# A delta-rule scan's triangular inverse cut into two pipeline stages, in 64-column form, and weight tiles' low parts kept in memory

## The chip, the cores and the metric

One NeuronCore of a Trainium2 chip. The metric is device time of one execution in microseconds; lower is better. A core has TensorE (matmuls; weight loads are listed apart), VectorE, ScalarE, GpSimd, and SyncE, which here only issues DMAs. Each takes its instructions in an order fixed when the program is built.

## The reference

One step of a two-layer hybrid decoder, for a prompt of 1024 tokens and for 8 samples of 8 tokens, width 1024. Layer 0 mixes with a convolution module, layer 1 with RWKV-7 time mixing; behind each mixer come attention over 256 memory tokens and a squared-ReLU MLP. The change touches layer 1's mixer:

```python
r = xr @ w_r; k = xk @ w_k; v = xv @ w_v        # x*: six mixes of a token and the token before it
decay, a, g = ...                                # each by a low-rank pair of products
def step(s, inp):                                # per head, s is 64 x 64; 16 heads
    rt, wt, kt, vt, at, bt = inp
    sa = einsum('bhvk,bhk->bhv', s, at)
    s = s * wt[:, :, None, :] + sa[..., None] * bt[:, :, None, :] + vt[..., None] * kt[:, :, None, :]
    return s, einsum('bhvk,bhk->bhv', s, rt)
```

## The kernel before, in words

**Two streams.** The tokens are cut into part 0 (512 prompt tokens) and part 1 (512 prompt tokens and the 64 of the samples). Stream A takes part 0 and stream B part 1 through the layers, each by a Python generator. `pace` advances whichever has the smaller clock; a generator yields an estimated cost, and the scan's bare yields count 1.344 (A) or 1.248 (B). This gives the written order, which is the priority by which the scheduler that builds the program places instructions; the scan's rank 1000 places further ahead (`SCAN_AHEAD`). A's scan must end before B's begins. Beside A's scan B does the end of its first MLP and its projections; beside B's scan A does its part of layer 1 up to the second MLP.

**Weights.** `Stream.load` brings a 128 x 1024 tile into one of four shared raw buffers (L110) and splits it: ScalarE's rounded copy is the high part (L95), VectorE's difference the low part (L96). A product takes three matmuls, high by high, high by low and low by high (L126 to L128). Each stream has a ring of two such tiles, `wt`; the next is loaded when one is taken. Both streams load and split the 24 tiles of w_r, w_k and w_v in `projections`.

**The scan.** It works on chunks of 64 tokens, eight for part 0, and the samples as one more and eight for part 1. `prep` loads a chunk (`ld`, one buffer, L1128), forms decayed keys and queries on VectorE, ScalarE and GpSimd (L1141 to L1178), multiplies them in four passes (L1199) whose results are copied out as `at`, `Aak` and `Aq` (L1202 to L1204), and then makes UV, BK, AV and `bon` (L1210 to L1233). `invert` inverts the unit-triangular 64 x 64 matrix `at` of each of 16 heads: `dg` (L1246, L1248) holds its diagonal 32 x 32 blocks, VectorE inverts the blocks of 16 (L1251 to L1288, giving `td`), and the blocks of 32 and 64 are joined by matmuls of 32 x 32 (L1302 to L1327); the result goes into a 128 x 128 block-diagonal `tt` for each pair of heads (L1329, L1333). `step` takes the state S (L1355), solves with `tt` (L1366) and updates S (L1373 to L1379); `finish` normalises and stores.

`run` works in stages. In each, `together` takes turns, a yield each, between `rest` (step and finish) of one chunk, `inverse` of the next and `prep` of the one behind it. All banks of PSUM that `prep`, `inverse` and the solution use are of one tag, `pp`, with two buffers (`bank("iv")` is one of them too).

Of the kernel before, what the change touches and what calls it, by code (L numbers as in the profile page):

```python
# [17 lines left out]
P = 128  # L18
D = 1024
NC8 = D // P  # L20
# [42 lines left out]
class Stream:  # L63


    def __init__(self, tc, nc, name, side, raw, width):
        self.tc, self.nc, self.name, self.side, self.raw, self.width = tc, nc, name, side, raw, width
        self.turn = self.loads = self.every = 0

# [28 lines left out]
    def load(self, src, cols=1024, rows=P, lo=None, slot=None):  # L98

        if slot is None:  # L100
            slot = self.ring[self.turn % len(self.ring)]
            self.turn += 1
# [9 lines left out]
        wt = pool.tile([P, 2, 1024], F32R, tag=tag, name="wt", bufs=n)  # L112
        self.loads += 1
        if self.every and self.loads % self.every == 0:
            lo = self.nc.gpsimd
        self.split(wt[:rows, 0, :cols], wt[:rows, 1, :cols], raw[:rows, :cols], lo)
        return wt
# [38 lines left out]
def body(tc, nc, es, a, o):  # L156
# [28 lines left out]
    scr = [[dram.tile([P, 6, n], F32, name=f"scr{i}_{m}") for m in range(NC8)] for i, (_, n, _) in enumerate(PARTS)]  # L185
    yg = [dram.tile([P, NC8, n], F32, name=f"yg{i}") for i, (_, n, _) in enumerate(PARTS)]
# [525 lines left out]
    def projections(s, ctx, part, h):  # L712
# [30 lines left out]
        weights = s.weights([(a["rw_w"][i, m], 1024, P) for i in range(3) for m in range(NC8)])  # L743
# [128 lines left out]
        yield from project(2, None, hidden(4, "a", [AF.Copy]), lora("gh", 5))  # L872
        yield from lora("a", 4)
# [193 lines left out]
BUF = dict(w=5, bon=2, at=2, ar=2, Aq=2, UV=2, AV=2, BK=2, pcs=3)  # L1067


def scan(tc, nc, a, o, s, ph, kept, env):  # L1070
# [25 lines left out]
    tts = [filled([P, 8, 128], f"tt{i}", 0.0) for i in range(2)]  # L1096
# [3 lines left out]
    dg = filled([P, 16, 32], "dgz", 0.0)  # L1100
# [29 lines left out]
    def prep(chunk):  # L1130
# [63 lines left out]
        for q in range(2):  # L1194
# [6 lines left out]
            for (h, hs), pa in zip(heads, pas):  # L1201
                nc.scalar.copy(at[hs, cs], pa[:64, :, :64])  # L1202
                nc.vector.tensor_tensor(Aak[64:, cs, h], pa[64:, :, :64], ms[64:], MUL)
                nc.vector.tensor_tensor(Aq[:, cs, h], pa[:, :, 64:], mi, MUL)  # L1204
                yield
# [28 lines left out]
        return dict(chunk=chunk, ar=ar, at=at, Aq=Aq, UV=UV, AV=AV, BK=BK, bon=bon, pcs=pcs)  # L1234
# [7 lines left out]
    def invert(at, tt, deep):  # L1242

        nc.scalar.copy(dg[:, :8], at[:, :, :32])  # L1246
# [42 lines left out]
        td = td[:, :8]  # L1289
# [4 lines left out]
        if deep:  # L1294
# [24 lines left out]
            X = new([P, 256], "W16").rearrange("p (i t) -> p i t", i=8)  # L1319
# [8 lines left out]
        for s in quads:  # L1328
            nc.scalar.copy(tt[s, :, s], td[s])  # L1329
        for h in range(2):  # L1330
            s, s1 = quads[2 * h], quads[2 * h + 1]
            if deep:
                nc.scalar.copy(tt[s, :, s1], pw[s])  # L1333
            else:
                nc.gpsimd.memset(tt[s, :, s1], 0.0)

    def solve(w, pz, cs, n):
# [5 lines left out]
        for g, c in enumerate(range(8)[cs]):  # L1343
            nc.tensor.matmul(pz[:, g, 64:128], lhsT=w["tt"][:, c], rhs=Z[:, g], start=True, stop=True)
# [4 lines left out]
    def step(w, py, S):  # L1349
# [15 lines left out]
        for i in range(8):  # L1365
            nc.tensor.matmul(pu[:, i], lhsT=w["tt"][:, i], rhs=Z[:, i], start=True, stop=True)  # L1366
# [77 lines left out]
    def inverse(n, w):  # L1444
        w["tt"] = tts[n % 2]
        yield from invert(w["at"], w["tt"], w["chunk"] is not None)
        yield
# [38 lines left out]
    def run(chunks):  # L1486
# [4 lines left out]
        if chunks[0] is None:  # L1491
            load_con("rst_s", "rst")
            w = yield from prep(None)
            load_con("rst_p", "rst")
            ready = yield from together(inverse(0, w), prep(chunks[1]))
            yield from together(rest(w), inverse(1, ready))
            n, chunks, ready, inverted = 2, chunks[2:], None, ready
            ready = yield from prep(chunks.pop(0))
        else:
            load_con("rst_p", "rst")  # L1500
        for chunk in chunks + [None, None]:
            gens = ([rest(inverted)] if inverted else []) + ([inverse(n, ready)] if ready else [])
            n += bool(ready)
            if chunk is not None:
                gens.append(prep(chunk))
# [145 lines left out]
```

## Time and profile before

| | |
|---|---|
| time, median of 3 runs | 3869.92 us (3869.62 to 3873.25) |
| the profiled execution's own time | 3869.88 us |
| its span | 3868.1 us |
| mean granted TensorE clock | 0.958 |
| TensorE busy | 3638.3 us (94%) |
| VectorE, ScalarE, GpSimd busy | 61%, 42%, 17% |

The span is from the first to the last instruction. The granted clock is a share of 2.4 GHz; the two levels are 2.4 and 1.2 GHz, and a figure between is a mean over time. Matmuls are pipelined, so that the durations of single ones overlap.

### The profile page before, as it was taken

Reading aid. Unit: us, or ns where it says so; the run is one execution under the profiler, and the core shown is the slowest. Engines: PE = TensorE matmul, PEld = TensorE weight load, DVE = VectorE, ACT = ScalarE, POOL = GpSimd, SP = SyncE. Lnnn points to the kernel's source line nnn. Section 1 sums busy time; section 2 is a strip of 40 time slices with the busy share of each in tenths; the row PEclk is TensorE's granted clock in tenths of the full one; section 3 lists DMA queues with packets and bytes.
Section 4 is the critical chain, followed back from the end, with each engine's and each line's share of the span. In section 5 each row is a group of like instructions: output and inputs, shape, how many; then the busy total and the mean of one; then the engine's idle time right before and its main releaser. Section 6 shows DMA issues by size and latency. Waiting matters only on the chain. (4 is left out here: it accounts for less than half of the span.)

```text
span 3868.1 us, 74950 instructions
## 1 busy us (share of the span) xinstructions
PE 3638.3 (94%) x30634; PEld 3386.9 (88%) x30634; DVE 2374.8 (61%) x4503; ACT 1614.7 (42%) x3180; POOL 669.6 (17%) x704
## 2 busy tenths in 40 slices
PE   8989979999999999999799888989999999989998
PEld 7767769999999999999688778768789999989998
DVE  7889964646545653437877635677874536553334
ACT  3223253445433454544556644344444335432222
POOL 0010031123201100012331201142232015101110
PEclk9989989999999999999799989889999999999998
DMA  6414213335422333343334365323324335422221
GB/s 224 131 55 130 80 62 105 102 121 166 153 88 88 110 114 123 121 131 95 84 103 110 84 217 177 105 69 78 77 75 128 121 107 191 143 77 82 83 82 63
DMA packets 323913, 430.81 MB, mean 111 GB/s; under 512 B 152304, under 2 KB 244720, under 8 KB 323568
## 3 DMA queue, kind: packets, MB, share of 16 engines
q1 hardware_dynamic: 295920, 399.25, 34.0%
q10 hardware_dynamic: 27648, 26.75, 2.0%
q8 instruction: 241, 3.95, 0.4%
q14 instruction: 104, 0.85, 0.1%
HBM read 356.53 MB, written 60.91 MB: 108 GB/s over the span
## 5 line engine op out<-in xcount | busy, mean ns | idle before, releaser
L96 DVE TENSOR_TENSOR wt<-raw,wt 128x1024 fp32r<-128x1024 f32 x471 | 592.8, 1262 | 505.7 <-ACT wt L95 499.9
L95 ACT CAST wt<-raw 128x1024 fp32r<-128x1024 f32 x512 | 533.2, 1046 | 509.1 <-PE B_d L128 245.7
L126 PE MATMUL B_d<-hAB,wt 128*128 128x288 f32 (+1 forms) x2240 | 672.9, 303 | 14.3 <-ACT wt L95 5.4
L126 PE MATMUL A_d<-hAA,wt 128*128 128x256 f32 x2240 | 640.2, 289 | 31.4 <-ACT wt L95 16.0
L127 PE MATMUL B_d<-hBB,wt 128*128 128x288 f32 (+1 forms) x2240 | 667.6, 299 | 2.2 <-DVE hBB L96 2.1
L128 PE MATMUL B_d<-hAB,wt 128*128 128x288 f32 (+1 forms) x2240 | 664.5, 298 | 0.3 <-DVE wt L96 0.3
L127 PE MATMUL A_d<-hBA,wt 128*128 128x256 f32 x2240 | 642.1, 288 | 5.2 <-DVE hBA L96 5.0
L128 PE MATMUL A_d<-hAA,wt 128*128 128x256 f32 x2240 | 634.9, 286 | 5.8 <-DVE wt L96 3.6
L126 PEld LDWEIGHTS A_d<-hAA,wt 128*128 128x128 f32 x2240 | 430.0, 193 | 43.6 <-ACT wt L95 19.3
L126 PEld LDWEIGHTS B_d<-hAB,wt 128*128 128x128 f32 x2240 | 424.4, 190 | 24.1 <-ACT wt L95 7.0
L127 PEld LDWEIGHTS A_d<-hBA,wt 128*128 128x128 f32 x2240 | 431.6, 193 | 15.5 <-DVE hBA L96 7.1
L128 PEld LDWEIGHTS A_d<-hAA,wt 128*128 128x128 f32 x2240 | 429.5, 193 | 13.0 <-DVE wt L96 4.6
L127 PEld LDWEIGHTS B_d<-hBB,wt 128*128 128x128 f32 x2240 | 425.8, 190 | 6.0 <-DVE hBB L96 3.2
L128 PEld LDWEIGHTS B_d<-hAB,wt 128*128 128x128 f32 x2240 | 425.0, 190 | 3.2 <-DVE wt L96 1.3
L694 POOL TENSOR_TENSOR t_sg<-t_ev 128x256 f32<-128x256 f32 (+1 forms) x256 | 183.4, 717 | 1406.8 <-ACT t_ev L692 1298.2
L126 PE MATMUL B_d<-u,wt 128*128 128x288 f32 x1024 | 305.4, 300 | 0.5 <-DVE xB L708 0.5
L128 PE MATMUL B_d<-u,wt 128*128 128x288 f32 x1024 | 302.5, 298 | 0.0
L127 PE MATMUL B_d<-u,wt 128*128 128x288 f32 x1024 | 302.3, 297 | 0.0
L126 PE MATMUL A_d<-u,wt 128*128 128x256 f32 x1024 | 288.6, 283 | 2.1 <-ACT wt L95 2.0
L128 PE MATMUL A_d<-u,wt 128*128 128x256 f32 x1024 | 289.3, 283 | 0.0
L127 PE MATMUL A_d<-u,wt 128*128 128x256 f32 x1024 | 288.6, 282 | 0.2 <-DVE u L96 0.2
L96 DVE TENSOR_TENSOR u<-t_sg,u 128x256 fp32r<-128x256 f32 (+1 forms) x256 | 134.3, 525 | 146.6 <-ACT u L95 145.9
(400 smaller groups left out, 7094.9 us busy)
## 6 DMA issues: line engine op xcount, KB each, us to landing
raw<-in_mlp_up_dram SPq DMA_DIRECT2D x128, 512.0 KB, 3.5
raw<-in_mlp_dn_dram SPq DMA_DIRECT2D x128, 512.0 KB, 3.5
raw<-in_rw_w_dram SPq DMA_DIRECT2D x64, 512.0 KB, 3.8
ld<-scr SPq DMA_DIRECT2D x136, 160.0 KB, 3.9
wf<-in_w_in_dram SPq DMA_DIRECT2D x32, 512.0 KB, 4.0
raw<-in_xa_w_q_dram SPq DMA_DIRECT2D x32, 512.0 KB, 3.5
raw<-in_xa_w_o_dram SPq DMA_DIRECT2D x32, 512.0 KB, 3.5
raw<-in_ck_dram SPq DMA_DIRECT2D x32, 512.0 KB, 3.5
```

Source lines behind the costliest of these rows:

```text
L95: self.nc.scalar.copy(hi, src)
L96: (engine or self.nc.vector).tensor_tensor(lo, src, hi.bitcast(F32), SUB)
L126: self.nc.tensor.matmul(out, lhsT=wh, rhs=mh, start=(i == 0), stop=False)
L127: self.nc.tensor.matmul(out, lhsT=wh, rhs=ml, start=False, stop=False)
L128: self.nc.tensor.matmul(out, lhsT=wl, rhs=mh, start=False, stop=(i == last))
L694: nc.gpsimd.tensor_mul(sg[:, :n], r[:, :n], r[:, :n])
```

## The change

- The inverse is cut in two. `blocks16` (up to `td`) is run by `begun` in turns with the chunk's own `prep`, from the yield at which `at` is complete. `blocks32` (the matmuls and `tt`) follows a stage later, where `inverse` stood. `dg` and `td` get two buffers each; the intermediate X uses the tag T32 in place of W16.
- `tt` is 64 columns wide, one block a head. The solution takes 16 matmuls of 64 x 64 in place of 8 of 128 x 128.
- A's first use of w_r, w_k and w_v writes each tile's low part to memory (`put`, ahead of the next load). B's use copies the high part and loads the low part, with no subtraction.

```diff
         self.turn = self.loads = self.every = 0
+        self.due = None
...
-    def load(self, src, cols=1024, rows=P, lo=None, slot=None):
+    def put(self):
+        if self.due:
+            dst, wt = self.due
+            self.nc.sync.dma_start(out=dst, in_=wt[:, 1].bitcast(F32))
+            self.due = None
+    def load(self, src, cols=1024, rows=P, lo=None, slot=None, share=None):
+        self.put()
         if slot is None:
...
         wt = pool.tile([P, 2, 1024], F32R, tag=tag, name="wt", bufs=n)
+        if share is not None and self.part:
+            self.nc.scalar.copy(wt[:, 0], raw)
+            self.nc.sync.dma_start(out=wt[:, 1].bitcast(F32), in_=share)
+            return wt
         self.loads += 1
...
         self.split(wt[:rows, 0, :cols], wt[:rows, 1, :cols], raw[:rows, :cols], lo)
+        if share is not None:
+            self.due = share, wt
         return wt
...
     scr = [[dram.tile([P, 6, n], F32, name=f"scr{i}_{m}") for m in range(NC8)] for i, (_, n, _) in enumerate(PARTS)]
+    low = [[dram.tile([P, 1024], F32, name=f"low{i}_{m}") for m in range(NC8)] for i in range(3)]
     yg = [dram.tile([P, NC8, n], F32, name=f"yg{i}") for i, (_, n, _) in enumerate(PARTS)]
...
         lora2 = {"w": a["w2"], "a": a["a2"], "g": a["g2"][:128], "h": a["g2"][128:]}
-        weights = s.weights([(a["rw_w"][i, m], 1024, P) for i in range(3) for m in range(NC8)])
+        weights = s.weights([(a["rw_w"][i, m], 1024, P, None, None, low[i][m]) for i in range(3) for m in range(NC8)])
...
         yield from project(2, None, hidden(4, "a", [AF.Copy]), lora("gh", 5))
+        s.put()
         yield from lora("a", 4)
...
 PE_PAIRS = (4, 3)
-BUF = dict(w=5, bon=2, at=2, ar=2, Aq=2, UV=2, AV=2, BK=2, pcs=3)
+BUF = dict(w=5, bon=2, at=2, ar=2, Aq=2, UV=2, AV=2, BK=2, pcs=3, td=2)
...
-    tts = [filled([P, 8, 128], f"tt{i}", 0.0) for i in range(2)]
+    tts = [filled([P, 8, 64], f"tt{i}", 0.0) for i in range(2)]
     Y32 = filled([P, 8, 32], "Y32", 0.0)
     E65 = filled([P, 8, 65], "E65", 1.0)
-    dg = filled([P, 16, 32], "dgz", 0.0)
+    dgs = [filled([P, 16, 32], f"dgz{i}", 0.0) for i in range(2)]
     d32 = filled([P, 32], "d32", 1.0)
...
-    def prep(chunk):
+    def prep(chunk, w):
...
                 nc.vector.tensor_tensor(Aq[:, cs, h], pa[:, :, 64:], mi, MUL)
-                yield
+                if (q, h) == (1, 1):
+                    w.update(chunk=chunk, at=at)
+                    yield "at"
+                else:
+                    yield
...
         nc.vector.tensor_tensor(bon, v, sb, MUL)
-        return dict(chunk=chunk, ar=ar, at=at, Aq=Aq, UV=UV, AV=AV, BK=BK, bon=bon, pcs=pcs)
+        w.update(ar=ar, Aq=Aq, UV=UV, AV=AV, BK=BK, bon=bon, pcs=pcs)
+        yield
...
-    def invert(at, tt, deep):
+    def blocks16(w, n):
+        at, deep = w["at"], w["chunk"] is not None
+        dg = w["dg"] = dgs[n % 2]
         nc.scalar.copy(dg[:, :8], at[:, :, :32])
...
         nc.vector.transpose(td.rearrange("p i (b t) -> p t (i b)", b=2), ts.rearrange("p t j s -> p t (j s)"))
-        td = td[:, :8]
+        w["td"] = td[:, :8]
+        yield
+    def blocks32(w, n):
+        at, td, dg, deep = w["at"], w["td"], w["dg"], w["chunk"] is not None
+        tt = w["tt"] = tts[n % 2]
...
                                      start=True, stop=True)
-            X = new([P, 256], "W16").rearrange("p (i t) -> p i t", i=8)
+            X = new([P, 8, 32], "T32")
             nc.scalar.copy(X[quads[1]], px[quads[1]])
...
                     nc.tensor.matmul(pw[quads[2 * h], i], lhsT=X[s, i], rhs=td[s, i], start=True, stop=True)
-        for s in quads:
-            nc.scalar.copy(tt[s, :, s], td[s])
         for h in range(2):
             s, s1 = quads[2 * h], quads[2 * h + 1]
+            nc.scalar.copy(tt[s, :, :32], td[s])
+            nc.scalar.copy(tt[s1, :, 32:], td[s1])
             if deep:
-                nc.scalar.copy(tt[s, :, s1], pw[s])
+                nc.scalar.copy(tt[s, :, 32:], pw[s])
             else:
-                nc.gpsimd.memset(tt[s, :, s1], 0.0)
+                nc.gpsimd.memset(tt[s, :, 32:], 0.0)
...
         for g, c in enumerate(range(8)[cs]):
-            nc.tensor.matmul(pz[:, g, 64:128], lhsT=w["tt"][:, c], rhs=Z[:, g], start=True, stop=True)
+            for h, s in heads:
+                nc.tensor.matmul(pz[s, g, 64:128], lhsT=w["tt"][s, c], rhs=Z[s, g], start=True, stop=True)
         nc.vector.tensor_copy(UV[:64, cs, 0], pz[:64, :, 64:128])
...
         for i in range(8):
-            nc.tensor.matmul(pu[:, i], lhsT=w["tt"][:, i], rhs=Z[:, i], start=True, stop=True)
+            for h, s in heads:
+                nc.tensor.matmul(pu[s, i], lhsT=w["tt"][s, i], rhs=Z[s, i], start=True, stop=True)
         nc.vector.tensor_copy(UV[:64, :, 0], pu[:64])
...
-    def inverse(n, w):
-        w["tt"] = tts[n % 2]
-        yield from invert(w["at"], w["tt"], w["chunk"] is not None)
-        yield
+    def begun(chunk, n):
+        w = {}
+        mine, other = prep(chunk, w), iter(())
+        while True:
+            c = next(mine, "end")
+            if c == "end":
+                break
+            if c == "at":
+                other = blocks16(w, n)
+            yield
+            if next(other, "end") != "end":
+                yield
+        for _ in other:
+            yield
+        return w
...
             load_con("rst_s", "rst")
-            w = yield from prep(None)
+            w = yield from begun(None, 0)
             load_con("rst_p", "rst")
-            ready = yield from together(inverse(0, w), prep(chunks[1]))
-            yield from together(rest(w), inverse(1, ready))
+            ready = yield from together(blocks32(w, 0), begun(chunks[1], 1))
+            yield from together(rest(w), blocks32(ready, 1))
             n, chunks, ready, inverted = 2, chunks[2:], None, ready
-            ready = yield from prep(chunks.pop(0))
+            ready = yield from begun(chunks.pop(0), 2)
         else:
...
         for chunk in chunks + [None, None]:
-            gens = ([rest(inverted)] if inverted else []) + ([inverse(n, ready)] if ready else [])
+            gens = ([rest(inverted)] if inverted else []) + ([blocks32(ready, n)] if ready else [])
             n += bool(ready)
             if chunk is not None:
-                gens.append(prep(chunk))
+                gens.append(begun(chunk, n))
             w = yield from together(*gens)
```

## Rows read from the trace of the kernel before

**Rows 1.** The page: busy time by engine, and 40 equal slices of the span, in tenths.

```profile
PE 3638.3 (94%) x30634; PEld 3386.9 (88%) x30634; DVE 2374.8 (61%) x4503; ACT 1614.7 (42%) x3180; POOL 669.6 (17%) x704
PE   8989979999999999999799888989999999989998
DVE  7889964646545653437877635677874536553334
...
PEclk9989989999999999999799989889999999999998
```

**Rows 2.** Busy time by stage; columns PE, PEld, DVE, ACT, POOL, clock, DMA, GB/s.

```profile
1300.00:1745.00 445.00, 444.51 (x3420) 440.81 (x3419) 212.97 (x412) 204.28 (x444) 33.25 (x49) 1.00 0.41 125
1745.00:2212.00 467.00, 424.29 (x4961) 371.67 (x4959) 367.62 (x811) 267.31 (x544) 122.71 (x105) 0.92 0.35 95
2212.00:2260.00 48.00, 28.40 (x180) 25.22 (x181) 14.40 (x12) 14.92 (x20) 9.34 (x5) 0.67 0.44 143
2212.00:2400.00 188.00, 160.46 (x1128) 150.77 (x1128) 70.07 (x103) 77.06 (x149) 14.61 (x14) 0.91 0.62 189
2450.00:2945.00 495.00, 457.49 (x5565) 395.87 (x5564) 351.39 (x715) 223.04 (x436) 148.21 (x124) 0.92 0.30 79
```

**Rows 3.** Waits of TensorE in scan A: total us, times, longest.

```profile
PE p_pp L1302 <- DVE Aq L1204: 5.8, 3, 3.5
...
PE p_pp L1366 <- ACT AV L1228: 4.6, 1, 4.6
...
PE p_pp L1317 <- DVE T L1312: 2.1, 1, 2.1
```

**Rows 4.** Waits of TensorE in scan B.

```profile
PE p_pp L1302 <- DVE Aq L1204: 3.3, 2, 2.1
```

**Rows 5.** Timeline of one chunk of scan A: start us, us, instruction.

```profile
2004.15 1.06 DVE L1288 STREAM_TRANSPOSE td<-M 128x512 f32<-128x512 f32 x1
...
2010.25 1.54 DVE L1141 TENSOR_TENSOR w<-ld,vec 128x512 f32<-128x512 f32 x1
...
2033.77 0.42 PE L1302 MATMUL p_pp<-T,dgz 32*32 32x16 f32 x17 [3.46 <-DVE Aq L1204]
...
2045.42 0.39 ACT L1246 COPY dgz<-at 128x256 f32<-128x256 f32 x1
...
2065.39 0.68 DVE L1233 TENSOR_TENSOR bon<-ld,p_pp 128x512 f32<-128x512 f32 x1
...
2075.67 0.69 DVE L1141 TENSOR_TENSOR w<-ld,vec 128x512 f32<-128x512 f32 x1 [1.07 <-DMA w<-in_lora_dram]
```

**Rows 6.** The line that begins a chunk, in scan A: duration ns, first and last start.

```profile
L1141 DVE TENSOR_TENSOR w<-ld,vec x8: 676/693/1537, 1747.8 to 2134.2; 128x512 f32<-128x512 f32 x8
```

**Rows 7.** Chain that ended last, in scan B: start us, us, matmuls.

```profile
2675.41 1.08 PE p_pp L1226 x32
...
2680.24 1.73 PE p_pp L1366 x16
```

**Rows 8.** ScalarE's copies of weights (page), and VectorE's subtractions in scan A.

```profile
L95 ACT CAST wt<-raw 128x1024 fp32r<-128x1024 f32 x512 | 533.2, 1046 | 509.1 <-PE B_d L128 245.7
...
L96 DVE TENSOR_TENSOR wt<-raw,wt x29: 1161/1221/2281, 1745.9 to 2177.0; 128x1024 fp32r<-128x1024 f32 x29
```

**Rows 9.** What SP's queue waited for in scan A.

```profile
SPq L788 <- PE B_hd L793: 113.1, 28, 20.6
SPq L110 <- DVE wt L96: 107.6, 13, 22.5
```

**Rows 10.** Loads of w_r, w_k, w_v: in 1300 to 1745, then in scan A.

```profile
L110 SPq DMA_DIRECT2D raw<-in_rw_w_dram x24: 327/328/350, 1301.3 to 1642.4; - x24
...
DMA to landing us min/median/max: 3.4/3.6/7.3
...
L110 SPq DMA_DIRECT2D raw<-in_rw_w_dram x18: 327/328/2013, 1807.3 to 2107.1; - x18
```

## Prediction

> **What bounds the kernel now.** I read the page's first two parts first. TensorE is busy for 3638.3 of 3868.1 us (94%), VectorE for 61% [rows 1]. The slice rows show where TensorE is not full: near the start, and in slices 19 to 30 of 40, where its granted clock falls to 7 or 8 tenths in four slices and VectorE is mostly at 6 to 8 tenths [rows 1]. These are the two scans, so I asked for busy time by stage [rows 2]. What a stage loses is its length less busy time times granted clock. From 1300 to 1745, where part A's projections run beside B's MLP, it loses 0.5 us of 445. In scan A (1745 to 2212) it loses 467 - 424.29 x 0.92 = 77 us, in scan B (2450 to 2945) 495 - 457.49 x 0.92 = 74 us, and in the short stretch behind scan A (2212 to 2260) 48 - 28.40 x 0.67 = 29 us. So TensorE is the bound, and what the change can win is TensorE work saved plus a part of some 180 us lost around the scans. Idle time alone is 42.7 us in scan A and 37.5 us in scan B; the lost time is 1.8 and 2.0 times that, because the granted clock is below 1.00 around the gaps.
>
> Then I read who is waited for on TensorE in both scans [rows 3, 4]. Much of it is the scan's own short matmuls, standing at the head of TensorE's queue. Those of the inverse and of the tail behind it come to 5.8 + 4.6 + 2.1 = 12.5 us in scan A [rows 3] and 3.3 + 2.1 = 5.4 us in scan B [rows 3, 4]: the row of L1317, 2.1 us, is the same in both scans and stands once.
>
> Last, one chunk in order of time [rows 5]. A chunk's tiles begin at 2010.25 (L1141) and the next chunk's at 2075.67; the eight of scan A come every (2134.2 - 1747.8) / 7 = 55.2 us [rows 6]. Two things are to be seen. The blocks of 16 already run in their chunk's own stage: the copy that begins them (L1246) stands at 2045.42, 35 us behind that chunk's start. And the finished td of the chunk before lies unused from 2004.15 + 1.06 to 2033.77, when L1302 gets its PSUM bank, released by Aq of the chunk in preparation. The two "pp" banks are shared by preparation, inverse and solution, so the larger blocks end up in the preparation's second half. That half ends with bon (L1233, 2065.39), which frees the one "ld" buffer for the next chunk.
>
> **The change part by part.**
>
> *The split.* All operations of the inverse stay. In the written order, blocks32 asks for its four banks in the first rounds of a stage, where preparation still works on VectorE and GpSimd and needs only one; from "at" on, preparation has the banks to itself. So I expect the 29 us wait of td to shrink and the waits named above to go in part: 12.5 x 1.8 + 5.4 x 2.0 = 33 us of lost time is what they cost. Preparation's first products then stand behind the inverse's banks, so I take half, -17 us. The ends are -33 and, as waits of half that size could as well appear anew on L1199, +17. Late next is preparation itself, whose VectorE share is unchanged. A second dg and td, and X in T32, only take away reuse: 0. One more yield a chunk (26 for 25) moves stream B's work by 8 x 1.344 = 10.8 us on the kernel's own clock; at scan A's loss rate of 77 / 467 = 0.165 that is 2 us either way, and I take 0.
>
> *The 64-column inverse.* Applying tt took 16 passes in 1.73 us; 32 passes of 64 by 64 with 64 columns (L1226) take 1.08 us [rows 7]. That is 0.65 us, 17 times (16 chunks; the samples in two halves): 11 us. With TensorE full for 92% of the scans I take -10 us; the ends are 0 (all in idle time) and -11. ScalarE's copies into tt stay six of the same shape, so 0.
>
> The Trainium skill speaks against this (TensorE: Matmul & The Clock Gate, section LDWEIGHTS): loading weights takes time by their columns. By that rule 32 loads of 64 columns cost what 16 of 128 do, the saving is nil and the sum below would be 3851 us. The row of the 128-column form agrees (1.73 / 16 = 0.108 us a pass; an estimate by the page's formula is 0.107), that of the 64-column form doesn't (1.08 / 32 = 0.034 us).
>
> *Low parts, first use (part A).* A still splits, and adds 24 writes of 512 KB on SP's queue, each waiting for VectorE's split and standing ahead of the next weight load. Of the loads there, SP already waits for such splits. A's 24 weight loads come every 341 / 23 = 14.8 us and land in 3.6 [rows 10]; one landing and split more (3.6 + 1.05 + 1.22 us, the last two ScalarE's copy and the subtraction [rows 8]) is under that, and TensorE is idle for 0.5 us there [rows 2]. I take 0. If the cover were gone, it would be one split per tile, 24 x 1.22 = 29 us at most; below nothing there is no reason, since nothing is removed.
>
> *Second use (part B).* 24 subtractions of 1.22 us leave VectorE, 18 of them in scan A's stretch, where 18 tiles are loaded [rows 8, 10]: 22 us of a VectorE that is busy for 368 of 467. At the loss rate of 0.165 that is -4 us; the ends are 0 and -22. The raw buffer comes free after ScalarE's copy. In exchange 24 loads of 512 KB go to SP's queue, and each waits there until TensorE has finished with the slot; behind it stand the scan's ld and gg loads and the hidden layers' w1. SP's nearest such stops, w1 for a matmul, are 113.1 / 28 = 4.0 us each [rows 9]. Queued loads cost nothing while the chunk's loads come early enough; the price if not is below. Six loads fall behind scan A, where DMA is at 0.62 share and 189 GB/s [rows 2]: 3.1 MB at 189 / 0.62 = 305 GB/s is 10 us of engine time against 0.38 x 188 = 71 us free. I take +2; the ends are 0 and +10.
>
> Sum: -17 - 10 + 0 - 4 + 2 = -29 us. The profiled execution took 3869.88 us (span 3868.1 and 1.8 around it), practically the median of 3869.92, so the forecast is **3841 us**.
>
> **The rivals.**
>
> *Only the arithmetic remains.* blocks32's four banks still pass through the same two, and L1302 merely trades places with L1199. For it: VectorE is busy for 368 of scan A's 467 us, so whoever holds the banks waits for it. Against it: td is ready 29 us early. Then it is -10 - 4 + 2, and 6 us of new waits, half of the 12.5 of [rows 3]: 3864 us, no change.
>
> *The banks free the whole chain.* If preparation no longer waits on the inverse, its tail loses L1317 to L1333, and the 29 us early td gives room; lost time in both scans halves, (77 + 74) / 2 = 75 us: 3795 us. For it: bon frees ld late, the next chunk starts behind that. Against it: VectorE is 79% busy in scan A, and B's own VectorE work is what feeds TensorE.
>
> *Slower: SP's queue.* A low part's load waits at SP's head for TensorE, and the chunk's ld and gg loads behind it come late. Two of them a chunk at 4.0 us (18 over 8 chunks) make scan A 8 x 8 = 64 us longer, at its loss rate 10.6 us lost. One more stop such as that behind scan A, where the other stream's weights come late too, is 29 us [rows 2]. With the -10 of the arithmetic this is +30 us: 3900 us. It decides once more than one such stop of 4 us per chunk stands ahead of ld. For it: SP is already stopped 107.6 and 113.1 us in scan A [rows 9]. Against it: it is also freed of 18 waits for VectorE's split.
>
> *Loading 64 columns twice saves nothing:* 32 passes then take the 1.73 us of 16, and the sum is without its -10: 3851 us. Against it stands [rows 7]. This is what the page's rule on weight loads would give.
>
> **How the numbers follow.** A change within 0.2% (8 us) can't be told from none. Main case 0.42 (own range 3820 to 3858), whole chain free 0.12, only the arithmetic 0.17, SP's queue 0.26, weight rule 0.03. Faster: nearly all of the main case and the chain and rule cases, and a quarter of the third: 0.60. Within: 0.12 of the third and 0.03 from the edges of others: 0.15. Slower: 0.25. The range goes from 3800, which leaves half of the chain case out, to 3890, which leaves out the upper part of SP's.
>
> **What would show it.** Right: the larger blocks' first matmul starts ahead of the next chunk's first L1199, not behind it; TensorE's waits on it for Aq are gone; chunk starts are nearer than 55 us; the solve's 32 passes take about 1.1 us; 24 subtractions fewer; the stretch of A's projections still full. Wrong: SP stopped longest at the low parts' loads, ld landing later behind bon, or a second stretch such as 2212 to 2260; or new waits of L1199 for blocks32's evacuations as large as those that went.

## The result, and the profile after

The changed kernel takes **3906.65 us** (median of 4 runs, 3905.98 to 3907.17), the kernel before beside it 3871.59 (4 runs, 3869.62 to 3878.71): a ratio of 1.0087, with an interval of 1.0074 to 1.0101. The forecast was 3841 us; the time is 35 us longer than before, and outside the range.

The page of the changed kernel, beside [rows 1]:

```profile
span 3905.4 us, 75648 instructions
...
PE 3675.4 (94%) x30906; PEld 3412.3 (87%) x30906; DVE 2356.9 (60%) x4479; ACT 1619.7 (41%) x3181; POOL 660.5 (17%) x706
...
PEclk9989989999999999999789898878899999999999
...
L97 DVE TENSOR_TENSOR wt<-raw,wt 128x1024 fp32r<-128x1024 f32 x447 | 563.9, 1264 | 495.9 <-ACT wt L96 479.2
```

The last row is VectorE's subtractions of weights, 447 of them, 24 fewer than before. The span grew by 37.3 us and TensorE's busy time by 37.1, so TensorE is idle as long as before: 3905.4 - 3675.4 = 230.0 us against 3868.1 - 3638.3 = 229.8 [rows 1]. It was busy for longer. Two things can do that, a lower granted clock and costlier instructions, and one sum tells them roughly apart: over slices of 5 us, busy time times granted clock is the work in full-clock time, and busy time times what the clock lacks to 1.00 is what I call the **low clock**. Work is 3519.4 us before and 3519.8 after; the low clock took 118.9 us before and 155.6 after. So the net difference of the two kernels, 36.7 us, is low clock. That the work is equal is no sign that nothing else changed: the 64-column form alone has 3505.7 (e5 below), so the rest of the change put some 14 us of work back. And the sum takes it that every pass goes at the clock, which a trace further down bears out only in part, so that it puts somewhat too much down to the clock. Nearly all of the difference lies in the scans; before 1745 us and behind 2990 us the two kernels lose the same to within 5 us.

By stage, beside [rows 2] (columns as there; the first five rows answer to those, the last two are stretches inside scan A):

```profile
1300.00:1745.00 445.00, 445.00 (x3425) 441.63 (x3425) 213.24 (x410) 205.34 (x444) 35.84 (x52) 1.00 0.50 155
1745.00:2205.00 460.00, 412.02 (x4891) 357.04 (x4889) 335.96 (x732) 244.00 (x483) 116.67 (x101) 0.87 0.38 105
2205.00:2260.00 55.00, 43.69 (x300) 38.08 (x301) 33.98 (x67) 34.52 (x73) 9.36 (x8) 0.91 0.58 186
2205.00:2400.00 195.00, 176.55 (x1203) 162.88 (x1204) 81.71 (x144) 99.81 (x202) 15.71 (x20) 0.94 0.70 222
2450.00:2945.00 495.00, 450.13 (x5424) 382.27 (x5425) 337.71 (x692) 217.28 (x424) 141.06 (x120) 0.87 0.28 74
2165.00:2170.00 5.00, 5.00 (x59) 4.56 (x58) 3.80 (x7) 3.34 (x7) 0.00 (x0) 1.00 0.38 97
2170.00:2195.00 25.00, 25.00 (x251) 19.27 (x250) 4.44 (x8) 4.17 (x11) 0.00 (x0) 0.66 0.12 43
```

Scan A now loses 460 - 412.02 x 0.87 = 102 us (77 before), scan B 495 - 450.13 x 0.87 = 103 us (74 before), the stretch between them 15 us (29 before). The last row is what to learn to see: by the profile TensorE is busy for all of 25 us, had been busy at full clock just before, and is granted 0.66 of its clock.

The split did in the trace what it was meant to do. One chunk's td and its first use, beside [rows 5], from two timelines:

```profile
2005.88 1.06 DVE L1314 STREAM_TRANSPOSE td<-M 128x512 f32<-128x512 f32 x1
...
2009.52 0.73 PE L1334 MATMUL p_pp<-T,dgz 32*32 32x16 f32 x64
```

td lies unused for 2.6 us instead of 29. Over the eight chunks of scan A it is 0.8 to 5.0 us, where it was 2.8 to 28.6: the chunk of [rows 5] was the longest of them. The line that begins a chunk (beside [rows 6]) now comes every (2121.5 - 1745.0) / 7 = 53.8 us instead of 55.2, and the solve's 32 passes take 1.08 us on the chain that ended last, instead of 1.73 (beside [rows 7], the same view):

```profile
L1159 DVE TENSOR_TENSOR w<-ld,vec x8: 655/693/951, 1745.0 to 2121.5; 128x512 f32<-128x512 f32 x8
```

```profile
2887.21 1.08 PE p_pp L1400 x32
```

Who is waited for on TensorE, in scan A and then in scan B, beside [rows 3, 4] (L1217 is the line that was L1199):

```profile
PE p_pp L1217 <- POOL bk L1192: 9.3, 2, 6.7
...
PE p_pz L1388 <- DVE S L1413: 6.0, 2, 3.0
...
PE p_pp L1217 <- DVE d L1205: 3.3, 1, 3.3
```

```profile
PE p_pp L1217 <- DVE Aq L1222: 13.8, 4, 8.9
...
PE p_pp L1217 <- POOL bk L1192: 2.6, 2, 1.3
```

The waits of the larger blocks for Aq are gone but for 0.6 us; waits of the next chunk's products on L1217 stand in their place: in the rows shown 12.6 us in scan A and 16.4 in scan B, where 12.5 and 5.4 were named. (Before, these products already waited 5.8 and 1.6 us in all.)

What stopped SP's queue in scan A, beside [rows 9] (L125 loads a low part):

```profile
SPq L1476 <- POOL y L1474: 82.0, 6, 28.1
SPq L805 <- PE B_hd L810: 66.9, 18, 20.9
SPq L125 <- PE B_d L144: 40.5, 8, 12.4
SPq L120 <- DVE wt L97: 40.5, 6, 9.7
```

The low parts' loads are not the longest stop, and the two stops of [rows 9] fell from 220.7 us to 107.4. The longest is now the store of a chunk's output y, which waits for GpSimd; before, its row was

```profile
SPq L1442 <- POOL y L1440: 22.0, 5, 6.2
```

So nearly all that the forecast named as signs of being right came true in the trace, the waits on L1217 are the one sign of being wrong, and the time moved the other way.

### The profile page after: what moved, and what is told of

The parts are those of the page before. It is cut to its first block, busy times and chain, and to the rows that moved or that the text cites. A ratio compares the mean times of both kernels' runs of the same rounds, so it can differ in the third digit from the quotient of the medians.

```text
span 3905.4 us, 75648 instructions
## 1 busy us (share of the span) xinstructions
PE 3675.4 (94%) x30906; PEld 3412.3 (87%) x30906; DVE 2356.9 (60%) x4479; ACT 1619.7 (41%) x3181; POOL 660.5 (17%) x706
## 4 chain that ended last, share of the span: by engine, by line
PE 75%; DVE 13%; ACT 5%; DMA 3%; issue 2%; SPq 1%; POOL 1%; ACTq 0%; DVEq 0%; POOLq 0%
PE B_d L142 10%; PE B_d L144 10%; PE B_d L143 10%; PE A_d L142 9%; PE A_d L143 9%; PE A_d L144 9%; PE A_d L362 3%; PE B_d L362 2%; PE p_pp L1217 2%; SPq L1146 1%; ACT wt L96 1%; DVE M L1305 1%; DVE wt L97 1%; PE A_hd L810 1%; DVE xB L461 1%
## 5 line engine op out<-in xcount | busy, mean ns | idle before, releaser
L97 DVE TENSOR_TENSOR wt<-raw,wt 128x1024 fp32r<-128x1024 f32 x447 | 563.9, 1264 | 495.9 <-ACT wt L96 479.2
L96 ACT CAST wt<-raw 128x1024 fp32r<-128x1024 f32 x488 | 508.7, 1046 | 495.8 <-PE B_d L144 259.4
L143 PEld LDWEIGHTS A_d<-hBA,wt 128*128 128x128 f32 x2240 | 432.3, 193 | 22.7 <-DVE hBA L97 11.5
```

The lines of the kernel that those rows point to most:

```text
L96: self.nc.scalar.copy(hi, src)
L97: (engine or self.nc.vector).tensor_tensor(lo, src, hi.bitcast(F32), SUB)
L143: self.nc.tensor.matmul(out, lhsT=wh, rhs=ml, start=False, stop=False)
```

## The experiments

The changed kernel counts 26 steps a chunk where the one before counts 25, and each step of a scan moves that stream's clock by SCAN_COST (1.344 in scan A, 1.248 in scan B) against the other stream's passes. I call what a chunk costs in this count the **pace**. Times are medians of 4 to 12 runs each (the kernel before took 3867 to 3872 beside them); idle time and low clock are from the one profiled execution, worked out as above, and that is one draw. The granted clock of the kernel before is 0.954 to 0.960 over its executions, 0.006 of 3868 us or some 23 us, so a difference in low clock of less than some 20 us between two kernels says little. e12's profiled execution (3868.6 us) is the slowest of its eight, e6's (3861.8) is 11.5 us under its median.

| kernel | time us | ratio to before | TensorE idle | low clock |
|---|---|---|---|---|
| before | 3869 | 1 | 229.8 | 118.9 |
| before, pace +1% (e10) | 3883.9 | 1.0022 to 1.0048 | 232.1 | 144.4 |
| before, pace +4% (e7) | 3903.3 | 1.0073 to 1.0098 | 229.4 | 157.4 |
| before, pace -4% (e9) | 3905.9 | 1.0083 to 1.0117 | 234.5 | 148.5 |
| before, 26 steps, same pace (e17) | 3871.4 | 1.0000 to 1.0018 | 226.0 | 129.9 |
| low parts alone (e6) | 3873.3 | 0.9998 to 1.0019 | 228.0 | 109.6 |
| 64 columns alone (e5) | 3854.6 | 0.9958 to 0.9976 | 223.1 | 131.1 |
| 64 columns, pace +1% (e14) | 3877.8 | 1.0011 to 1.0028 | 237.7 | 128.6 |
| 64 columns, pace -1% (e18) | 3888.0 | 1.0041 to 1.0068 | 242.3 | 135.7 |
| low and 64 (e1) | 3885.4 | 1.0026 to 1.0058 | 243.6 | 129.8 |
| low and 64, pace -1% (e16) | 3879.1 | 1.0007 to 1.0025 | 233.9 | 137.4 |
| split and 64 (e2) | 3889.1 | 1.0042 to 1.0079 | 235.5 | 140.6 |
| split and 64, pace restored (e12) | 3862.0 | 0.9968 to 0.9989 | 212.3 | 138.9 |
| split and 64, pace -6% (e15) | 3903.0 | 1.0072 to 1.0099 | 243.9 | 159.3 |
| the same as e12, groups apart (e13) | 3880.3 | 1.0017 to 1.0041 | 241.1 | 143.9 |
| the whole change | 3906.7 | 1.0074 to 1.0101 | 230.0 | 155.6 |
| whole, groups apart (e3) | 3906.0 | 1.0083 to 1.0115 | 248.7 | 153.3 |
| whole, groups mixed more (e4) | 3938.9 | 1.0167 to 1.0199 | 219.3 | 191.8 |
| whole, pace restored (e8) | 3884.6 | 1.0031 to 1.0055 | 226.2 | 139.3 |
| whole, pace -8% (e11) | 3883.3 | 1.0020 to 1.0046 | 213.8 | 147.4 |

**First theory: alternating tile shapes.** In the changed kernel's trace the larger blocks' 32 by 32 matmuls (L1334) are issued in turn with the step's 128-row ones (L1407), one pair by one pair. A timeline of scan B:

```profile
2632.03 0.33 PE L1407 MATMUL p_pz<-UV,BK 128*64 128x64 f32 x2
2632.29 0.23 PE L1334 MATMUL p_pp<-T,dgz 32*32 32x16 f32 x2
2632.45 0.33 PE L1407 MATMUL p_pz<-UV,BK 128*64 128x64 f32 x2
2632.71 0.23 PE L1334 MATMUL p_pp<-T,dgz 32*32 32x16 f32 x2
```

A round of two pairs takes 2632.45 - 2632.03 = 0.42 us; in one block, 64 matmuls of L1334 take 0.73 us (above), so two take 0.02, and 32 of L1407 with 32 of the next line take some 2 us where they stand in a block, so two take some 0.07. Two such stretches, from 2170.85 and from 2630.6, last 16 and 14 us. The Trainium skill says why a change of shape is not free (TensorEngine Tiling (Array Packing), section Key Properties): a change of the tiling mode drains TensorE. The trace agrees as far as the price goes: 0.33 of the 0.42 us go with the two changes. Further on in the first stretch the granted clock is 0.50, and a round takes 0.62 us:

```profile
2175.69 0.28 PE L1334 MATMUL p_pp<-T,dgz 32*32 32x16 f32 x2
...
2176.31 0.28 PE L1334 MATMUL p_pp<-T,dgz 32*32 32x16 f32 x2
```

At half the clock a round takes 0.62 / 0.42 = 1.5 times as long and not twice; that is where the sum above counts too much as low clock. Rivals to this theory: the low parts' queue, and a clock that falls with the small tiles of the 64-column form.

*e1_low64_no_split*: the kernel before, with these two edits of the change (cut short; `put`, the load of a low part and the narrower `tt` belong to them) and not the split:

```
-        weights = s.weights([(a["rw_w"][i, m], 1024, P) for ...
+        weights = s.weights([(a["rw_w"][i, m], 1024, P, None, None, low[i][m]) for ...
...
-            nc.tensor.matmul(pu[:, i], lhsT=w["tt"][:, i], rhs=Z[:, i], ...)
+            for h, s in heads:
+                nc.tensor.matmul(pu[s, i], lhsT=w["tt"][s, i], rhs=Z[s, i], ...)
```

> The kernel before with the 64-column inverse and the low parts kept in memory, without the split in two stages. Order theory (the split lets the 32x32 matmuls of the larger blocks alternate one by one with the step's 128x64 matmuls, in stretches of 16.07 and 14.48 us where the same matmuls in two blocks take some 3 us): no such stretch, so 3855 to 3868 us (the arithmetic's -10 us, and a few us of VectorE). SP theory (low parts' loads stop SP's queue): about 3895 us or more, since all 24 loads are in. Clock theory (64x64 matmuls keep TensorE's granted clock low): 3885 us or more, with the clock of both scans under the 0.92 of before.

Measured 3885.4: half of the loss is there without the split and without the long alternations. A miss for the order theory; the clock theory's number is hit, but e5 below rules that theory out.

*e2_split_no_low*: the changed kernel with the first of these lines as before. Part B makes its 24 subtractions itself again.

> The changed kernel with every low part made by VectorE again (no writes, no loads of them). Order theory: the built order still holds one alternating stretch of 24 switches (55 and 48 in the changed kernel), so about half of the loss stays: 3875 to 3895 us. SP theory: the loss goes, 3860 us or less. Clock theory: nothing changes, 3900 us.

Measured 3889.1, inside the order theory's range. So the 64-column form together with either of the other two parts is about 20 us slower than before.

*e3_groups_apart* and *e4_groups_worse*: the changed kernel, with an order given between the step's matmuls and the larger blocks': in both the step stands behind the blocks' first group; in e3 the blocks' second group stands behind the whole step as well. e4 lacks this second order, and as built has seven long alternations where the changed kernel has two. Neighbouring passes that change between 32 x 32 and 128 x 64 number 143 in the changed kernel's trace, 25 in e3's, 264 in e4's, and 17 in the trace of the kernel before.

```
+    with behind(gate.pop("st", None)):           # e3: second group of blocks32 behind the step's last matmul
         nc.tensor.matmul(pt[s, i, 16:], lhsT=Y32[s, i], rhs=td[s, i, 16:], ...)
...
+    with behind(gate.pop("mm", None)):           # e3 and e4: the step behind the first group of blocks32
         nc.tensor.matmul(pz[s, i], lhsT=w["BK"][:, i, h], rhs=UV[:, i, h], ...)
```

> The changed kernel, with the matmuls of the larger blocks' first group, the step's update and the larger blocks' second group queued on TensorE one group behind the other (order of issue only, no work changed). Order theory: the two long stretches lose 26 us against the same matmuls apart (39.2 us in four stretches less 4 x 3.2), and the clock falls less behind them: 3870 to 3885 us. SP and clock theories: within 8 us of 3906.

> The changed kernel, with the step's update queued behind the larger blocks' first group alone. The built order then holds seven stretches in which the second group alternates with the step's products, of 21 to 43 switches, 213 in all, where the changed kernel has two of 55 and 48. Order theory: at (16.07 + 14.48 - 6.4) / 103 = 0.23 us a switch that is 49 us instead of 24, so about 3930 us. SP and clock theories: within 8 us of 3906.

e3 took 3906.0 us, as long as the changed kernel. Its work fell by 20 us, from 3519.8 to 3499.7, so the alternations did cost that; but idle time rose by 19. e4 took 3938.9, near the order theory's 3930, with the lowest clock of all kernels: work rose by 7 us and low clock by 36. Alternations cost, and to take them out in this way gave nothing back. With e1, the theory falls as the whole cause of the loss; what it has to do with the split's share comes with e12.

**Second theory: the pace.** By the slices of 5 us, e1 loses 22 us more than before in scan B and 6 in scan A, and in scan B no low part is loaded (the last goes out at 2321.0). So something that reaches both scans must differ, such as the order in which the two streams are interleaved, and I tried each edit alone, and the pace alone.

*e5_64_alone*: the kernel before, with the second edit of e1's diff.

> The kernel before with the 64-column inverse alone. Built to split the 18 us that the 64-column inverse and the low parts cost together without the pipeline split (3885). Filler theory (the time lost in the second scan goes with the stretches in which only the scan's own small matmuls stand on TensorE and none of the other part's 128x128x256 passes; gaps over 4 us sum to 74 us before, 92 in that run, 114 after): the order of the work hardly moves, so 3862 to 3875. Small-tile theory (two 64x64 passes in place of one 128x128 let the granted clock fall): the 18 us are here, 3880 to 3890. Queue theory (the low loads and the puts on SP's queue are what costs): within 4 us of 3867.

*e6_low_alone*: with the first one.

> The kernel before with the low parts kept in memory alone. Queue theory: the 18 us are here, 3880 to 3890, with SP's waits on the low loads' buffers longest in the first scan stretch. Small-tile theory: within 4 us of 3867. Filler theory: 24 subtractions fewer move the order of the planner's work a little, 3862 to 3880, and what is lost is lost in the second scan, where no low load stands.

The 64-column form alone is faster by 14 us (ratio 0.9967). Low parts alone are no change. Their loads do stop SP's queue in scan A:

```profile
SPq L120 <- DVE wt L97: 53.4, 7, 12.4
SPq L805 <- PE B_hd L810: 51.7, 23, 14.9
SPq L125 <- PE B_d L144: 44.9, 6, 19.7
```

That is as much as in the changed kernel (40.5), and by itself it costs nothing: the queue theory falls for the low parts alone. The small-tile theory falls with e5, which gains where that theory lost.

*e7_before_pace_up_4pct*, the kernel before, and *e8_after_pace_restored*, the changed one:

```
-SCAN_COST = [1.344, 1.248]
+SCAN_COST = [1.398, 1.298]      # e7: 25 steps cost what 26 do
+SCAN_COST = [1.292, 1.2]        # e8: 26 steps cost what 25 did
```

> A control: the kernel before with the scan's cost per step set up by 26/25 (1.398 and 1.298), which is what one more step per chunk in the changed scan does to the pace between the scan and the other part; no instruction is added or taken away. Filler theory: the pace alone moves the time by 8 us or more, and the lost time of the second scan goes with its gaps without filler. Queue and small-tile theories, and the theory that the alternations of 32-row and 128-row tiles cost it: within 4 us of 3867.

> The changed kernel with the scan's cost per step set down by 25/26 (1.292 and 1.200), so that a chunk of 26 steps costs what one of 25 did before. Filler theory: part of the 39 us comes back, 3870 to 3895. Queue and small-tile theories: 3902 to 3910. Alternation theory: the built order holds longest alternations of 27 and 23 switches where the changed kernel has 55 and 48, some 10 to 15 us less, 3890 to 3897.

With no instruction added, e7 is 35 us slower than before: as much as the changed kernel loses, and again as low clock and not as idle time. Its page, and three windows of scan B:

```profile
span 3897.1 us, 74970 instructions
...
PE 3667.7 (94%) x30634; PEld 3408.9 (87%) x30634; DVE 2393.2 (61%) x4503; ACT 1617.5 (42%) x3179; POOL 662.2 (17%) x704
```

```profile
2755.00:2765.00 10.00, 5.05 (x68) 3.82 (x64) 10.00 (x13) 3.78 (x7) 6.08 (x5) 0.94 0.31 105
2765.00:2800.00 35.00, 33.57 (x355) 27.71 (x357) 27.39 (x77) 18.85 (x42) 8.42 (x8) 0.53 0.07 17
2800.00:2810.00 10.00, 10.00 (x100) 9.12 (x98) 9.49 (x26) 4.48 (x10) 1.33 (x2) 1.00 0.68 133
```

Idle is 3897.1 - 3667.7 = 229.4 us, as before; busy time grew by 29.4. In the windows TensorE is idle for 5 us, and then goes at 0.53 of its clock for 35 us in which it is busy for 33.57. The rows of that stretch, by line:

```profile
L1199 PE MATMUL p_pp<-ar,bk 64*128 64x128 f32 x32 | 6.6, 443 | 0.0
L126 PE MATMUL A_d<-hAA,wt 128*128 128x256 f32 x15 | 5.9, 419 | 0.0
...
L1317 PE MATMUL p_pp<-T,at 32*32 32x32 f32 x32 | 2.1, 240 | 0.0
...
L1302 PE MATMUL p_pp<-T,dgz 32*32 32x16 f32 x64 | 1.6, 212 | 0.0
```

Most passes there are the scan's own small ones, with few of the other stream's 128x128x256 passes among them (15, 14 and 14 of its three lines, of 355). e8 gave 22 of the changed kernel's 38 us back.

*e9_before_pace_down_4pct* (1.292 and 1.200), *e10_before_pace_up_1pct* (1.357 and 1.260), *e11_after_pace_down_8pct* (1.240 and 1.152):

> The kernel before with the scan's cost per step set down by 25/26 (1.292 and 1.200): the other side of the control that cost 35 us. Pace theory (the time is a smooth function of the pace between the scan and the other part's passes, with its best near the pace of the kernel before): 3867 to 3885, for a step off the best to the other side. Chance theory (any move of the planner's order deals the waits and the clock anew, some 20 us either way, whatever its direction): anywhere from 3850 to 3905. If the kernel before stands on a slope and not at a best: below 3860.

> The kernel before with the scan's cost per step up by 1% (1.357 and 1.260). Pace theory: a quarter of the 35 us of the 4% at most, 3865 to 3878. Chance theory: as far off as the large step, 10 us or more to either side.

> The changed kernel with the scan's cost per step at 1.240 and 1.152, one more step of 4% in the direction that gave 22 us back. Pace theory: with the pace of the kernel before best for the changed kernel too, 3885 to 3905; if the pipelined scan wants a faster pace than the old one (the larger blocks now stand ahead), 3860 to 3880. Chance theory: anywhere from 3860 to 3910.

Off its pace by 4% to the other side the kernel before is 37 us slower, and 1% up costs 15. Of the four paces tried the one it has is the best by far, and its low clock, 118.9 us, is lower than in any kernel here but e6. e9 and e10 are both more than the smooth pace theory allowed; the chance theory's ranges hold e10 and, but for 1 us, e9. e11 falls between the pace theory's two cases: a pace 4% further down changes nothing.

*e12_split_no_low_pace_restored*: e2 with the pace of e8.

> The changed kernel without the low parts in memory (each part makes its own subtractions, as before) and with the pace set back by 25/26; beside the 64-column inverse alone (3855) it shows what the two-stage inverse does at the pace of before. If the split is worth what was forecast (-17) and only the pace spoilt it: 3835 to 3845. If it is worth nothing: 3850 to 3860. If its order costs by itself (alternations of tile shapes, the new waits): 3865 to 3885.

Measured 3862.0, between the second case and the third: 27 us come back, and it beats the kernel before by 0.2%, but stays 7 us behind the 64-column form alone. Its page:

```profile
span 3866.8 us, 75525 instructions
...
PE 3654.5 (95%) x30906; PEld 3395.8 (88%) x30906; DVE 2382.3 (62%) x4503; ACT 1619.7 (42%) x3181; POOL 658.6 (17%) x706
```

Idle is 3866.8 - 3654.5 = 212.3 us and low clock 138.9. What the split alone did is read beside e5, which has the 64-column form too and whose profiled execution also lies 7 us above its median: idle time is 10.8 us less, but low clock is 7.8 more (within the spread) and work 9.9 more, 3515.6 for 3505.7. Together that is the 6.9 us between the two profiled spans. Where the work comes from stands in the rows of the 1024 passes that begin the larger blocks and of the first 512 of the step's update, over the whole span, in e5, e12 and e13 (e13 is e12 with the order of e3):

```profile
L1375 PE MATMUL p_pz<-UV,BK 128*64 128x64 f32 x512 | 26.2, 244 | 1.6 <-DVE UV L1369 1.4 <-ACT UV L1370 0.2
...
L1302 PE MATMUL p_pp<-T,dgz 32*32 32x16 f32 x1024 | 17.1, 183 | 10.8 <-DVE Aq L1204 10.7
```

```profile
L1407 PE MATMUL p_pz<-UV,BK 128*64 128x64 f32 x512 | 32.1, 233 | 1.3 <-DVE UV L1401 1.1 <-ACT UV L1402 0.2
...
L1334 PE MATMUL p_pp<-T,dgz 32*32 32x16 f32 x1024 | 30.2, 188 | 0.0
```

```profile
L1414 PE MATMUL p_pz<-UV,BK 128*64 128x64 f32 x512 | 23.2, 255 | 0.0
...
L1336 PE MATMUL p_pp<-T,dgz 32*32 32x16 f32 x1024 | 16.4, 188 | 8.5 <-DVE nt L234 5.6 <-DVE T L1331 2.9
```

The split takes the blocks' wait for Aq away, 10.8 us to 0.0, and the same passes then keep TensorE busy for 30.2 us instead of 17.1, because they now meet the step's: changes between the two shapes number 9 in e5's trace, 116 in e12's, 29 in e13's. (In alternation the busy times of the two rows overlap, so that their growth isn't to be added up.)

*e13_split_groups_apart_pace_restored*: e12 with the order of e3, as said. *e14_64_alone_pace_up_1pct* and *e18_64_alone_pace_down_1pct*: e5 at 1.357 and 1.260, and at 1.330 and 1.235. *e15_split_no_low_pace_down_6pct*: e2 at 1.264 and 1.175. *e16_low64_pace_down_1pct*: e1 at 1.330 and 1.235.

> Split and 64-column inverse, no low parts in memory, pace set back by 25/26, and the 32-row matmuls of the larger blocks issued behind the step's 128-row ones instead of in turn with them (63 switches of shape left in the built order of 180). Beside the same kernel without that order (3862). Alternation theory: the switches that go are worth 10 to 15 us of TensorE work, 3847 to 3853. If waits take their place, as they did at the unrestored pace: 3858 to 3880.

> The 64-column inverse alone, at a pace up by 1%, where the kernel before costs 3884. If the 14 us of that edit are arithmetic on TensorE, they stay at every pace: 3865 to 3875. If its 3855 was a lucky order: 3875 to 3895.

> Split and 64-column inverse, no low parts, pace at 1.264 and 1.175 (6% below the changed kernel's; at 4% below it is 3862, at the unchanged pace 3889). If the split's best pace lies lower, because the larger blocks no longer wait: 3840 to 3858. If the pace of before is its best: 3862 to 3880.

> 64-column inverse and low parts without the split, at a pace 1% down (at the pace of before it costs 3885, where the 64-column inverse alone takes 3855 and the low parts alone 3873). If the 31 us are the order that the low parts shift, a small move of the pace re-deals them: 3855 to 3873 or 3890 to 3905. If they are work or waits of the low parts beside the narrower inverse: 3880 to 3890.

> The 64-column inverse alone at a pace 1% down (3855 at the pace of before, 3878 at 1% up). Chance theory: 3860 to 3890, TensorE's full-clock work again near 3506. If the family only has another best pace, on this side: below 3855.

e13 took 3880.3 us and repeats e3 at the restored pace: TensorE is busy for 18 us less than in e12, and idle for 29 us more. Page, then its waits in scan B:

```profile
span 3877.3 us, 75560 instructions
...
PE 3636.2 (94%) x30906; PEld 3381.2 (87%) x30906; DVE 2384.3 (61%) x4503; ACT 1615.0 (42%) x3178; POOL 657.7 (17%) x706
```

```profile
PE p_pp L1217 <- POOL bk L1192: 9.4, 3, 4.5
...
PE p_pp L1217 <- DVE d L1205: 6.1, 1, 6.1
```

e12 has 4.7 and 1.9 us of these. e14 is 6 us faster than the kernel before at the same pace, where the arithmetic's case asked for 9 to 19. With e18 the 64-column form, too, is best at the pace of before, of the three tried (23 and 33 us worse to either side); e18 is inside the chance theory's range, with its work at 3506.5 us as that theory said. e15 is slower than either of its cases: 2% of pace below e12 costs 41 us. e16 lies between its cases; at a pace 1% down, low parts and 64 columns are 9 us faster than 64 columns alone, at the pace of before 31 us slower.

*e17_before_26_steps*: the kernel before with one `yield` more behind each inverse, and e8's SCAN_COST.

```
         yield from invert(w["at"], w["tt"], w["chunk"] is not None)
         yield
+        yield
```

> The kernel before with one empty step more behind each inverse, as a chunk of the changed kernel has (26 instead of 25), and the cost per step set down by 25/26, so that a chunk counts as much as before. No instruction, tile or transfer changes; only the order in which the same work is interleaved. Chance theory (any move of the order deals the clock and the waits of the scans anew, and the kernel before is a good draw): slower by 8 to 35 us, 3877 to 3905, with the difference in low clock rather than idle time. Pace theory (only the cost of a chunk matters): 3865 to 3875.

Measured 3871.4, no change: an empty step costs nothing once the pace is put right. e9 and e17 have the same SCAN_COST and differ by this one empty step alone, 3905.9 us against 3871.4, so one step in 25 is worth 34 us in this kernel. Against the chance theory the run says less. Counted in the traces, the number of the other stream's passes that stand ahead of a pass of the scan differs from the kernel before by 10 on average in e17, by 50 in e10, 65 in e7 and 96 in e9, so e17's order hardly moved. In e6 it differs by 34, and nothing is lost, so a moved order need not cost. Shown is that the pace moves the time; whether the pace of before is best for a reason, or was a good draw, isn't.

## Why the prediction was wrong, step by step

**The steps that failed.** The edits, taken one after the other along the runs, add up to the 38 us between the kernel before (3868.8) and the changed one (3906.7):

| term of the forecast | forecast us | measured us | from the runs |
|---|---|---|---|
| 64-column form | -10 | -14 | before to e5 |
| split | -17 | +7 | e5 to e12 |
| low parts | -4 + 2 + 0 | +23 | e12 to e8 |
| one step more a chunk | 0 | +22 | e8 to the whole |

Three of the four terms failed, by 24, 25 and 22 us. In another order of the edits the shares would differ: without low parts the step is worth 27 (e2 to e12).

**The step more, 0.** "One more yield a chunk (26 for 25) moves stream B's work by 8 x 1.344 = 10.8 us on the kernel's own clock; at scan A's loss rate of 77 / 467 = 0.165 that is 2 us either way, and I take 0." The yield shifts both scans against the other stream's passes, in every chunk, and the sentence counts scan A alone. The same 4% of pace on the kernel before costs 35 us (e7), one empty step more or less 34 (e9 to e17); put right on the changed kernel, it gives 22 back (e8). The loss rate of the stage was no measure for it: the average of a stage says nothing of its neighbours.

**The split, -17.** The mechanism was right as far as it went: the larger blocks start 3 us behind td, chunks come nearer, and the idle time went much as forecast (half of the 17.9 us named is 9; beside e5, 10.8 are gone). Two things failed. "All operations of the inverse stay" put the order in which they meet the step's at nothing; the alternation costs 9.9 us of work, and taken out (e13) it leaves waits that cost more. And I took lost time to be 1.8 to 2.0 times idle time, so that idle time saved would save low clock too; low clock did not fall (131.1 in e5, 138.9 in e12). The rival "only the arithmetic remains" had the new waits on L1217 in the right place and their size too small; the main case allowed for them in its range, and not in its number.

**The 64-column form, -10.** Right in direction and nearly in size: 14 us at the pace of before (e5), 6 at 1% up (e14). The 32 passes take 1.08 us as the sum had it, 0.65 less than before, 17 times; what goes beyond that 11 us isn't explained. By the Trainium skill's rule (TensorE: Matmul & The Clock Gate, section LDWEIGHTS) the form would be worth nothing, and the trace speaks against that.

**Low parts, -4 + 2 + 0.** Alone they change nothing that can be told from none: 3873.3 against 3868.8, a ratio of 0.9998 to 1.0019 (e6). Part A's stretch stayed full, 445.00 of 445.00 us. Beside the other edits they cost 18 us (e2 to the whole), 23 (e12 to e8) and 31 (e5 to e1), and in one pair gain 9 (e18 to e16). So it is no fixed price of the transfers. What makes it is open; between e12 and e8 idle time differs by 14 us and the low clock not at all, and a few per cent of pace move these kernels by as much.

**SP's queue** as a rival gave 3900 us, near the measured time. That is luck: low parts alone have its stops and not its loss (e6), and the low parts' loads are not SP's longest stop. That the queue makes the 18 to 31 us that they cost beside the other edits isn't ruled out.

**What stays open.** Why so small a change of pace costs so much isn't shown, nor what the low parts cost beside the other edits. That the clock falls where the scan's small matmuls stand with few full-size passes among them is read from the stretches above and from e4; no run changes that alone. Low parts on another queue weren't tried, nor a finer search of the pace for the changed kernel: of the three it was run at, 3883.3 is the best. The version to keep is the kernel before with the 64-column form alone, 3854.6 us: it beats both, at the pace of before.

## What to carry to other kernels

Where an order is built from a cost per step, count the steps that an edit adds or drops, and correct the cost before anything else is priced: here one step in 25 was worth 22 to 35 us, about as much as the whole forecast gain of 29. Run the kernel before a per cent off its constants: how far its time moves (15 us here) is the least that an edit must be worth before a single build can judge it. And split busy time into full-clock work and low clock, beside a kernel with the same instructions: an engine that is busy longer at the same idle time is not waiting for anybody, and here a wait taken away came back as work.

## What the runs showed of the hardware

The granted clock fell to its lower level with TensorE busy throughout by the profile: in the changed kernel 25.00 of 25.00 us at a mean of 0.66, behind a stretch at 1.00; in its 5 us slices from 2175 to 2190 the granted clock is 0.50, the lower level of 1.2 GHz. What went just before was the alternation of 32 x 32 and 128 x 64 passes from 2170.85. The Trainium skill (TensorE: Matmul & The Clock Gate, section HAM oscillation — how this bites in real kernels) warns of idle gaps. The profile shows none in this stretch, so a busy TensorE in the profile is no proof of full clock. Across the kernels here low clock (109.6 to 191.8 us) does not go with idle time (212.3 to 248.7): the kernel with the lowest clock, e4, is among those with the least idle time. A change between 32 x 32 and 128 x 64 passes cost some 0.16 us at full clock (0.33 for two), and a round of two changes took 0.42 us at full clock and 0.62 at half.
